# A hybrid diffusion step on one core: query-key norm sums in pool ps2, a weight slot released later, two adaLN slabs moved to the bank change

## The chip, the cores and the metric

The kernel runs on one core of a Trainium2 chip. The metric is the device time of one execution in microseconds (us); the time given for a kernel is the median of its runs. TensorE is called PE here, VectorE DVE, ScalarE ACT, GpSimd POOL and SyncE SP, as in the profile.

## The reference

One inference step of a network of two layers on 640 tokens of width 1024: 512 of a sample and 128 of a prompt. Each layer is FFN1 (SwiGLU, 2816 wide), a mixer, FFN2; each is preceded by a norm that is modulated by `shift`, `scale` and followed by a `gate` (adaLN: nine vectors per layer, from `silu(cond) @ w_ada + b_ada`).

```python
x = x + 0.5 * gate1 * swiglu(mod(rmsnorm(x)))
x = x + gate2 * mixer(mod(rmsnorm(x)))
x = x + 0.5 * gate3 * swiglu(mod(rmsnorm(x)))
# mixer of layer 0
q, k, v, xb, gb = split(h @ w_in)            # 5 x 512 columns
q = rms_norm(q per head of 64, q_g) / 8;  k = rms_norm(k per head of 64, k_g)
y = concat(attention(q, k, v), rglru(xb) * gelu(gb)) @ w_out
# mixer of layer 1: real part of a 2-D DFT, then @ w_out
```

The change lies in layer 0: the norm of `q` and `k`, the opening of the mixer and its out projection.

## The kernel before

**Tiling.** The channels lie on the 128 partitions; the tokens are two halves of 320 (`HT`). Every product of activations and weights is computed from a high and a low part of each operand, as three matmuls (`mm3`, L276 to L284, PE's line L283: high by high, low by high, high by low). A weight unit of 128x1024 arrives by a transfer from SP in a staging buffer `st`, ACT copies its high part (`whi`, L177), DVE subtracts for the low part (`wlo`, L182). Which unit is split when is decided by `prep`, `unit` and `done`: `done` gives a weight slot back, and the split of the next unit is issued there.

**Order.** Nothing reorders the program: each engine runs its instructions in the order in which the Python code issues them, and a wait of one instruction holds all behind it on its engine.

**adaLN.** `w_ada` comes in 144 slabs of 128x1024. `fill` (L312) issues the four matmuls of a slab (L329), which add to an accumulator `ada_ps`, a bank of `ps2`. Eight slabs make one modulation vector; after the eighth, `ada_finish` evacuates the accumulator on ACT (`adaev`, L342), and `ada_end` (L355), called at the next use of any such vector or two slabs later, turns it by two transposes on PE (`adaT`). Slabs are spread over the program by calls of `fill`, as filler for PE. FFN1 of layer 0 ends with 44 used; attention takes up to number 80.

**PSUM.** Of eight banks, pool `ps2` has two, which `bank2` (L105) hands out in turn to the accumulator, norm sums and others; pool `ps` has six, as six single banks or, after `psum(True)` (L92), as three pairs. The mixer of layer 0 runs with pairs.

**The mixer of layer 0** (`mixer0`). FFN1 ends in `down_last`: 16 products `pd` (two halves by eight blocks of 128 channels), each added to `x` on DVE by `x_update` (L383) and followed by the step of the next norm that `after` issues. In the second half every second block hands its weight slot back with `done`. Then the projection: 20 units of `w_in` in the order `IN_ORDER`, each a pair of banks `pj`, one for each half of the tokens. The first three units run together for the first half while the norm of the second half is computed (`norm_a`: sums `nst` on PE, L404, then on DVE from L417 on; `norm_b`). After a unit its evacuation is issued. For `q` and `k` that is `qk_norm` (L1089), a generator: it copies and squares on ACT, and later, in the middle of another unit, issues on PE a sum of squares over each head's 64 channels for either half (`ss`, a product with the block matrix `bones`, L1102), on ACT a table load, Ln and Exp (L1103 to L1107), on POOL a square (L1108), and on DVE (L1110 to L1121) the rest. There are eight such pairs of sums, four of `q` and four of `k`. Between them run the steps of the recurrent unit `lru` (L1037, gates on PE at L1050). After the projection comes `attention` (L1277), with the first blocks of the out projection at its end (`out_ahead` L910, `out_last` L933). Between these two the pool `ps` changes back to single banks: this is the bank change.

Of the kernel before, what the change touches and what calls it, by code (L numbers as in the profile page):

```python
# [11 lines left out]
AF = mybir.ActivationFunctionType  # L12
ALU = mybir.AluOpType
# [9 lines left out]
HT = 320  # L23
SPL = TS - HT
EPS = 1e-6
# [17 lines left out]
class Kern:  # L43
# [687 lines left out]
    def ffn_body(self, l, i, fills, qfills, after, mid, late):  # L731
        nc = self.nc
        gate = self.gate(l, i)
        self.begun = None

        def evac(f, h, pg, pu):
            sg = self.t2.tile([P, HT], F32, tag="y", name="sg", bufs=3)
            nc.scalar.activation(out=sg, in_=pg[:, :HT], func=AF.Silu)
            nc.vector.tensor_tensor(out=sg, in0=sg, in1=pu[:, :HT], op=ALU.mult)
            self.g_split(f, h, sg)  # L740

        def step(n):
            for _ in range(n):
                next(norm, 0)

        if fills:
            us = [self.unit() for _ in range(4)]
            for h in range(2):
                ps = [self.bank("pg") for _ in us]
                for n, j in self.mm_side([p[:, :HT] for p in ps], us, h, 0 if h else LAG):  # L750
                    if j == 3 and h == 0 and n < 4 and (l, i) != (1, 2):
                        self.flush()
                        self.load()
                    elif j == 3:
                        self.prep(self.n_use + 1, 1)
                    if j == 3 and h == 0:
                        if n == 1:
                            if not self.normed:
                                self.norm_a(1)
                            norm = self.norm_steps(1, l, i, True)  # L760
                        elif n == 4:
                            step(3)
                    elif j == 3:
                        step(1)
                        if n < 4:
                            self.fill(fills.pop(0))
                    if (n, j, h) == (EQ, 3, 1):
                        self.quad(2, 0, True)
                    if (n, j, h) == (6, 3, 1):
                        step(9)  # L770
                        self.t_end()
                    if n == 6 and j % 2:
                        evac(j // 2, h, *ps[j - 1:j + 1])
                    if n == 6 and h:
                        self.done(MOST)
                step(2)
            step(9)
            self.t_end()
        else:
            self.ffn_start(evac)  # L780
        f = 2
        for bi, nb in enumerate(BLK):
            end = min(sum(BLK[:bi + 1]) + 1, NF)
            while f < end:
                self.quad(f, qfills.pop(0))
                next(mid, None)
                f += 1
            if bi == 0:
                self.ada_end()
            fs = range(sum(BLK[:bi]), sum(BLK[:bi + 1]))  # L790
            if bi == len(BLK) - 1:
                if late:
                    late()
                self.down_last(fs, gate, after)
            else:
                for c in range(0, KD, 2):
                    w = self.unit()
                    for j in range(2):
                        for h in range(2):
                            p = self.bank("pd")  # L800
                            self.down(p, w, j, h, fs, fs)
                            self.x_update(h, c + j, p, gate)
                    self.done()
# [3 lines left out]
        self.mm3(p[:, 0:HT], w, k, [self.gpart(f, h) for f in now], first=now[0] == fs[0],  # L807
                 last=now[-1] == fs[-1])

    def down_last(self, fs, gate, after):  # L810


        ws = [self.unit() for _ in range(4)]
        self.prep(self.n_use + self.LS)
        order = [(h, c) for h in range(2) for c in range(8)]
        ps = {}
        for n, (h, c) in enumerate(order):
            if n < 4:
                ps[n] = self.bank("pd")
                self.down(ps[n], ws[c // 2], c % 2, h, fs, fs[:-1])  # L820
        for n, (h, c) in enumerate(order):
            p = ps.pop(n, None)
            if p is None:
                p = self.bank("pd")
                self.down(p, ws[c // 2], c % 2, h, fs, fs)
            else:
                self.down(p, ws[c // 2], c % 2, h, fs, fs[-1:])
            self.x_update(h, c, p, gate)
            after(h, c)
            if h and c % 2:  # L830
                self.done()

    def quad(self, f, fills, begin=False):

# [75 lines left out]
    def out_ahead(self, gate, after):  # L910

        (w, p), v = self.ahead, self.unit()
        b = self.pair("w1")

        def end(h):
            self.mm3(p[:, h, 0:HT], w, (3,), [self.h[h][3]], first=False)
            self.x_update(h, 0, p[:, h], gate)
            after(h, 0)

        def whole(h):  # L920
            ks = (7, 6, 5, 4, 0, 1, 2, 3)
            self.mm3(b[:, h, 0:HT], v, ks, [self.h[h][k] for k in ks])
            self.x_update(h, 1, b[:, h], gate)
            after(h, 1)

        end(0)
        whole(0)
        end(1)
        self.done()
        whole(1)  # L930
        self.done()

    def out_last(self, xs, gate, after, c0=0):  # L933
# [155 lines left out]
    def qk_norm(self, which, c, ps):  # L1089

        nc, t2 = self.nc, self.t2
        raw, sq, y = [None] * 2, [None] * 2, [None] * 2
        for h in range(2):
            raw[h] = t2.tile([P, HT], F32, tag=f"acc{h}", name="raw", bufs=1)
            sq[h] = t2.tile([P, HT], F32, tag="sq", name="qsq")
            nc.scalar.activation(out=raw[h], in_=ps[:, h, 0:HT], func=AF.Copy)
            nc.scalar.activation(out=sq[h], in_=raw[h], func=AF.Square)
        yield
        yield
        ss = self.pair("ss")  # L1100
        for h in range(2):
            nc.tensor.matmul(ss[:, h, 0:HT], lhsT=self.bones, rhs=sq[h], start=True, stop=True)  # L1102
        nc.scalar.preload_act_table_set("natural_log_exp_and_others")  # L1103
        for h in range(2):
            y[h] = t2.tile([P, HT], F32, tag="y", name="qy", bufs=3)
            nc.scalar.activation(out=y[h], in_=ss[:, h, 0:HT], func=AF.Ln, scale=1.0 / 64, bias=self.eps)
            nc.scalar.activation(out=y[h], in_=y[h], func=AF.Exp, scale=-0.5)  # L1107
            nc.gpsimd.tensor_tensor(out=sq[h], in0=y[h], in1=y[h], op=ALU.mult)  # L1108
        for h, r0, r1 in ((0, 0, 5), (1, 5, 8)):
            nc.vector.scalar_tensor_tensor(out=sq[h], in0=ss[:, h, 0:HT], scalar=64 * EPS, in1=sq[h], op0=ALU.add, op1=ALU.mult)  # L1110
            nc.vector.tensor_scalar(out=sq[h], in0=sq[h], scalar1=-0.5 / 64, scalar2=1.5, op0=ALU.mult, op1=ALU.add)
            nc.vector.scalar_tensor_tensor(out=y[h], in0=raw[h], scalar=self.qk_g[:, which:which + 1], in1=y[h],
                                           op0=ALU.mult, op1=ALU.mult)
            m = 64 * (r1 - r0)
            if which == 0:
                v = lambda t: t[:, 0:m].rearrange("p (r j c) -> p r j c", j=4, c=16)
                o = self.qs[c][:, 0:TS].rearrange("p (j r c) -> p r j c", j=4, c=16)[:, r0:r1]
            else:
                v = lambda t: t[:, 0:m].rearrange("p (r c) -> p r c", c=64)
                o = self.kt[c][:, r0:r1, 8:72]  # L1120
            nc.vector.tensor_tensor(out=o, in0=v(y[h]), in1=v(sq[h]), op=ALU.mult)  # L1121
        o = self.qs[c][:, TS:] if which == 0 else self.kp[c]
        nc.vector.tensor_tensor(out=o, in0=y[1][:, SPL:], in1=sq[1][:, SPL:], op=ALU.mult)
# [153 lines left out]
    def attention(self, early):  # L1277
        nc, ap, nb, cks, cvs = self.nc, self.ap, self.nb, self.cks, self.cvs
# [89 lines left out]
        for s in range(n + 3):  # L1368
            if 0 <= s - 2 < n:
                B(*tiles[s - 2])  # L1370
            self.fill(min(1, 80 - self.s_use))
            if 0 <= s - 1 < n:
                N(*tiles[s - 1])
            if s < n:
                c, j = tiles[s]
# [8 lines left out]
                    if j == 3:  # L1384
                        self.cache_load(c + 1)
            next(early, None)
            self.fill(min(1, 80 - self.s_use))
            if s >= n and s - n < 2:
                ahead(s - n)
            if 0 <= s - 3 < n:  # L1390
# [477 lines left out]
```

## Time and profile before

| | us |
|---|---|
| median of 3 runs (2276.57 to 2277.95) | 2277.17 |
| the profiled execution | 2276.42 |
| its span in the profile | 2274.6 |
| PE busy | 2219.0 (98%) |
| PE's weight loads | 2106.3 (93%) |
| DVE busy | 1539.6 (68%) |
| ACT busy | 993.2 (44%) |
| POOL busy | 949.1 (42%) |

The mean granted clock of PE is 0.995 of full speed. Of the span, 1.8 us of the profiled execution's time lie outside it. Matmuls overlap in the records, so a row of PE can last longer than the step to the next one. An "x4" behind a row counts the records that it groups; a float32 matmul that is not split leaves two records.

### The profile page before, as it was taken

How to read it: one execution, taken by the hardware profiler on the slowest of the kernel's cores; microseconds unless marked ns; L12 is line 12 of the kernel's file. 1: busy time of each engine (PE TensorE's matmuls, PEld its weight loads, DVE VectorE, ACT ScalarE, POOL GpSimd, SP SyncE). 2: the span in 40 equal slices, each digit the busy share in tenths (PEclk: the TensorE clock that was granted, in tenths of full speed). 3: DMA queues.
4: the chain of work that ended last, by engine and by line, in shares of the span. 5: the costliest groups of instructions: out<-in, count | busy, mean ns of one | idle time of the engine just before them, and what ended most of it. 6: DMA issues, size and time to landing. Idle time of an engine off the chain costs nothing.

```text
span 2274.6 us, 39868 instructions
## 1 busy us (share of the span) xinstructions
PE 2219.0 (98%) x15534; PEld 2106.3 (93%) x15534; DVE 1539.6 (68%) x2871; ACT 993.2 (44%) x1792; POOL 949.1 (42%) x830
## 2 busy tenths in 40 slices
PE   7999999999999999999999999999999999999999
PEld 5899999999995889999999989999999889999999
DVE  6777677666865368666666786666667777666665
ACT  4433333357766444333333453333335453333332
POOL 2544544440023235444444454444443744444441
PEclk9999999999999999999999999999999999999999
DMA  7432333311229333233322243223231422222221
GB/s 291 138 119 88 102 101 107 119 65 57 65 80 320 102 135 107 102 108 107 99 98 82 94 148 130 96 100 112 101 104 54 139 84 84 82 79 84 84 91 56
DMA packets 75508, 245.44 MB, mean 108 GB/s; under 512 B 8884, under 2 KB 13236, under 8 KB 75320
## 3 DMA queue, kind: packets, MB, share of 16 engines
q1 hardware_dynamic: 74168, 241.28, 31.2%
q8 instruction: 123, 2.02, 0.3%
q10 hardware_dynamic: 1152, 1.61, 0.2%
q14 instruction: 65, 0.53, 0.1%
HBM read 239.71 MB, written 3.15 MB: 107 GB/s over the span
## 4 chain that ended last, share of the span: by engine, by line
PE 80%; DVE 11%; ACT 5%; issue 2%; POOL 2%; DMA 0%; ACTq 0%; DVEq 0%; SPq 0%; POOLq 0%
PE q L283 40%; PE pd L283 26%; PE pj L283 5%; PE ada L329 2%; DVE wlo L182 2%; DVE tl L173 1%; PE pg L283 1%; DVE hl L501 1%; ACT hh L487 1%; PE gt L1050 1%; PE pos L1599 1%; DVE x L383 1%; PE w L283 1%; PE S L1303 1%; PE PT L1329 0%
## 5 line engine op out<-in xcount | busy, mean ns | idle before, releaser
L182 DVE TENSOR_TENSOR wlo<-st,whi 128x1024 fp32r<-128x1024 f32 (+2 forms) x401 | 500.3, 1258 | 17.3 <-ACT whi L177 16.7
L177 ACT ACTIVATE whi<-st 128x1024 fp32r<-128x1024 f32 (+2 forms) x405 | 398.5, 991 | 216.2 <-POOL st L233 141.6
L283 PE MATMUL pd<-g,whi 128*128 128x320 f32 x1536 | 347.4, 311 | 2.1 <-DVE x L383 2.0
L383 DVE SCALAR_TENSOR_TENSOR x<-pd,mods,x 128x320 f32<-128x320 f32 (+2 forms) x690 | 260.9, 431 | 96.2 <-PE pd L283 95.9
L283 PE MATMUL q<-hh,whi 128*128 128x320 f32 x960 | 300.9, 313 | 1.0 <-DVE u L838 1.0
L283 PE MATMUL q<-hh,wlo 128*128 128x320 f32 x960 | 296.8, 309 | 2.9 <-DVE wlo L182 2.9
L283 PE MATMUL q<-th,whi 128*128 128x320 f32 x960 | 297.2, 310 | 2.3 <-DVE sg L838 2.3
L283 PE MATMUL q<-th,wlo 128*128 128x320 f32 x960 | 296.5, 309 | 0.0
L283 PE MATMUL q<-hl,whi 128*128 128x320 f32 x960 | 296.3, 309 | 0.0
L283 PE MATMUL q<-tl,whi 128*128 128x320 f32 x960 | 296.1, 308 | 0.0
L838 POOL TENSOR_TENSOR u<-u,u 128x320 f32<-128x320 f32 x80 | 106.0, 1325 | 423.1 <-DVE u L838 369.5
L232 POOL TENSOR_TENSOR st<-sums,st 128x512 f32<-128x512 f32 x80 | 125.0, 1563 | 368.6 <-DVE wlo L182 359.2
L283 PEld LDWEIGHTS pd<-g,whi 128*128 128x128 f32 x1536 | 256.8, 188 | 6.6 <-DVE x L383 3.0
L283 PE MATMUL pd<-g,wlo 128*128 128x320 f32 x768 | 236.9, 308 | 0.0
L283 PE MATMUL pd<-hh,whi 128*128 128x320 f32 x736 | 229.1, 311 | 0.9 <-DVE x L383 0.9
L283 PE MATMUL pd<-hl,whi 128*128 128x320 f32 x736 | 227.8, 310 | 0.0
L283 PE MATMUL pd<-hh,wlo 128*128 128x320 f32 x736 | 227.6, 309 | 0.0
L283 PEld LDWEIGHTS q<-hh,whi 128*128 128x128 f32 x960 | 180.2, 188 | 17.0 <-issue 9.9
L839 ACT ACTIVATE sg<-sg 128x320 f32<-128x320 f32 x160 | 75.4, 471 | 271.7 <-DVE sg L838 271.7
L283 PEld LDWEIGHTS q<-th,whi 128*128 128x128 f32 x960 | 180.2, 188 | 5.6 <-issue 3.2
L283 PEld LDWEIGHTS q<-hh,wlo 128*128 128x128 f32 x960 | 180.2, 188 | 3.7 <-DVE wlo L182 3.7
L283 PEld LDWEIGHTS q<-th,wlo 128*128 128x128 f32 x960 | 180.4, 188 | 0.0
(339 smaller groups left out, 5013.0 us busy)
## 6 DMA issues: line engine op xcount, KB each, us to landing
st<-w_ada SPq DMA_DIRECT2D x144, 512.0 KB, 4.9
st<-ffn_gate SPq DMA_DIRECT2D x88, 512.0 KB, 3.5
st<-ffn_up SPq DMA_DIRECT2D x88, 512.0 KB, 3.6
st<-ffn_down SPq DMA_DIRECT2D x96, 384.0 KB, 3.0
st<-w_in SPq DMA_DIRECT2D x20, 512.0 KB, 3.5
st<-ffn_down SPq DMA_DIRECT2D x16, 512.0 KB, 3.5
st<-w_out_ab SPq DMA_DIRECT2D x8, 512.0 KB, 3.7
st<-w_out_c SPq DMA_DIRECT2D x8, 512.0 KB, 3.5
```

Of the source, the lines that this page charges most:

```text
L173: (eng or self.nc.vector).tensor_tensor(out=lo, in0=src, in1=hi.bitcast(F32), op=ALU.subtract)
L177: self.nc.scalar.activation(out=hi, in_=src, func=AF.Copy)
L182: self.low.tensor_tensor(out=lo, in0=src, in1=hi.bitcast(F32), op=ALU.subtract)
L232: self.nc.gpsimd.tensor_tensor(out=s[:, 0:512], in0=it.s1, in1=s[:, 0:512], op=ALU.subtract)
L283: self.nc.tensor.matmul(out, lhsT=l, rhs=r, start=first and j == 0, stop=last and j == len(ops) - 1)
L329: nc.tensor.matmul(self.ada_ps[32 * j:32 * j + 32, 0:256], lhsT=self.s_sb[:, k, :], rhs=t[:, 256 * j:256 * j + 256], start=k == 0, stop=k ...
L383: self.nc.vector.scalar_tensor_tensor(out=self.x[h][c][:, sl], in0=ps[:, sl], scalar=gate[:, c, r:r + 1], in1=self.x[h][c][:, sl], op0=ALU ...
L487: nc.scalar.activation(out=hi, in_=y, func=AF.Copy)
L501: (self.nc.vector if h or c % 2 else self.nc.gpsimd).tensor_tensor(out=hl, in0=y, in1=hh.bitcast(F32), op=ALU.subtract)
L838: tt = lambda e, o, a, b, op=ALU.add: e.tensor_tensor(out=o, in0=a, in1=b, op=op)
L839: cp = lambda o, p, fn=AF.Copy: nc.scalar.activation(out=o, in_=p, func=fn)
L1050: nc.tensor.matmul(g[:, s, 0:322], lhsT=wt[:, d, j, :], rhs=xc[:, 322 * s:322 * s + 322], start=True, stop=True)
```

## The change

Three edits.

1. In `qk_norm` the two sums of squares, one for each half of the tokens, are no longer the two banks of a pair of pool `ps`, but two tiles of one bank each from `ps2`, by `bank2`.
2. In `down_last`, only in FFN1 of layer 0, the third hand-back of a weight slot in the second half (block 5) is left out and made up for at the end.
3. In attention the slabs go up to number 78 in place of 80; slabs 78 and 79 are issued in `out_ahead`, behind its last product.

```diff
-                self.down_last(fs, gate, after)
+                self.down_last(fs, gate, after, l == i == 0)
...
-    def down_last(self, fs, gate, after):
+    def down_last(self, fs, gate, after, hold=False):
...
-            if h and c % 2:
+            if h and c % 2 and (c != 5 or not hold):
                 self.done()
+        if hold:
+            self.done()
...
         whole(1)
+        self.fill(2)
         self.done()
...
-        ss = self.pair("ss")
+        ss = [self.bank2("ss") for _ in range(2)]
         for h in range(2):
-            nc.tensor.matmul(ss[:, h, 0:HT], lhsT=self.bones, rhs=sq[h], start=True, stop=True)
+            nc.tensor.matmul(ss[h][:, 0:HT], lhsT=self.bones, rhs=sq[h], start=True, stop=True)
...
-            nc.scalar.activation(out=y[h], in_=ss[:, h, 0:HT], func=AF.Ln, scale=1.0 / 64, bias=self.eps)
+            nc.scalar.activation(out=y[h], in_=ss[h][:, 0:HT], func=AF.Ln, scale=1.0 / 64, bias=self.eps)
...
-            nc.vector.scalar_tensor_tensor(out=sq[h], in0=ss[:, h, 0:HT], scalar=64 * EPS, in1=sq[h], op0=ALU.add, op1=ALU.mult)
+            nc.vector.scalar_tensor_tensor(out=sq[h], in0=ss[h][:, 0:HT], scalar=64 * EPS, in1=sq[h], op0=ALU.add, op1=ALU.mult)
...
-            self.fill(min(1, 80 - self.s_use))
+            self.fill(min(1, 78 - self.s_use))
```

The last pair of lines stands twice in `attention`. The line numbers of the changed kernel are those of before, plus 1 from L811 on, plus 3 from L832 and plus 4 from L931: the sums at L1102 are now at L1106, DVE's first read of them moves from L1110 to L1114.

**The sums, on PE.** The first of the eight pairs, in the middle of the fourth unit of the projection; `ss` are the sums, `pj` the projection. Each row names in brackets the engines and transfer queues that its instruction waits for. Before:

```order
L283 MATMUL pj_5288<-hh7_101,wlo1_70 128x320
L1102 MATMUL ss_5540<-qsq_5465,bones_5228 128x320 [waits DMAHW4_49,DMAHW2_49,DMAHW5_49,DMAHW1_49,DMAHW7_49,DMAHW0_49,Activation_49]
L1102 MATMUL ss_5540<-qsq_5469,bones_5228 128x320 [waits Activation_49]
L283 MATMUL pj_5561<-hh0_87,whi0_67 128x320 [waits PE_49,Activation_49]
L283 MATMUL pj_5561<-hl0_88,whi0_67 128x320
```

Now:

```order
L283 MATMUL pj_5288<-hh7_101,wlo1_70 128x320
L1106 MATMUL ss_5540<-qsq_5465,bones_5228 128x320 [waits DMAHW2_49,DMAHW4_49,DMAHW1_49,DMAHW5_49,DMAHW0_49,DMAHW7_49,PE_49,Activation_49]
L1106 MATMUL ss_5541<-qsq_5469,bones_5228 128x320 [waits DVE_49]
L283 MATMUL pj_5562<-hh0_87,whi0_67 128x320
L283 MATMUL pj_5562<-hl0_88,whi0_67 128x320
```

The second sum waits for DVE in place of ACT, and the second half of the unit follows behind it. The accumulator `ada_4264` is the tile of `ps2` that is open meanwhile: its last slab before the projection, and its first one after, which is in attention, stand in PE's order now as they did before:

```order
L329 MATMUL ada_4264<-st0_157,s_sb_112 32x256 [waits Pool_49]
L329 MATMUL ada_4264<-st0_157,s_sb_112 32x256
```

```order
L329 MATMUL ada_4264<-st2_66,s_sb_112 32x256 [waits DMAHW4_49]
L329 MATMUL ada_4264<-st2_66,s_sb_112 32x256 x3
```

**The opening, on DVE.** The last norm steps of FFN1's end and the low half of two weight units; `hl` is the low part of the normed input, `x` the residual. Before:

```order
L498 SCALAR_TENSOR_TENSOR hl_94<-y,mods,hh_93 128x320
L182 TENSOR_TENSOR wlo_70<-st_64,whi_69 128x1024
L383 SCALAR_TENSOR_TENSOR x_86<-pd,mods,x_86 128x192
L383 SCALAR_TENSOR_TENSOR x_86<-pd,mods,x_86 128x128
L475 SCALAR_TENSOR_TENSOR y<-x_85,sc,nbc 128x320
L383 SCALAR_TENSOR_TENSOR x_86<-pd,mods,x_86 128x192
L383 SCALAR_TENSOR_TENSOR x_86<-pd,mods,x_86 128x128
L479 TENSOR_TENSOR y<-x_85,nbc 128x320
L498 SCALAR_TENSOR_TENSOR hl_98<-y,mods,hh_97 128x320
L475 SCALAR_TENSOR_TENSOR y<-x_85,sc,nbc 128x320
L498 SCALAR_TENSOR_TENSOR hl_102<-y,mods,hh_101 128x320
L182 TENSOR_TENSOR wlo_68<-st_66,whi_67 128x1024
```

Now:

```order
L498 SCALAR_TENSOR_TENSOR hl_94<-y,mods,hh_93 128x320
L383 SCALAR_TENSOR_TENSOR x_86<-pd,mods,x_86 128x192
L383 SCALAR_TENSOR_TENSOR x_86<-pd,mods,x_86 128x128
L475 SCALAR_TENSOR_TENSOR y<-x_85,sc,nbc 128x320
L383 SCALAR_TENSOR_TENSOR x_86<-pd,mods,x_86 128x192
L383 SCALAR_TENSOR_TENSOR x_86<-pd,mods,x_86 128x128
L479 TENSOR_TENSOR y<-x_85,nbc 128x320
L498 SCALAR_TENSOR_TENSOR hl_98<-y,mods,hh_97 128x320
L475 SCALAR_TENSOR_TENSOR y<-x_85,sc,nbc 128x320
L498 SCALAR_TENSOR_TENSOR hl_102<-y,mods,hh_101 128x320
L182 TENSOR_TENSOR wlo_70<-st_64,whi_69 128x1024
L182 TENSOR_TENSOR wlo_68<-st_66,whi_67 128x1024
```

`wlo_70` has moved from between the norm steps to behind the last of them, next to `wlo_68`. On ACT one split (`whi_67`) moves in the same way behind its last norm step for that half. On PE the projection opens with three units in turn, and `wlo_70` is read by its ninth matmul, here the third row:

```order
L283 MATMUL pj_5288<-hh0_87,whi1_69 128x320 [waits Activation_49]
L283 MATMUL pj_5288<-hl0_88,whi1_69 128x320
L283 MATMUL pj_5288<-hh0_87,wlo1_70 128x320 [waits DVE_49]
L283 MATMUL pj_5286<-hh1_89,whi2_71 128x320
L283 MATMUL pj_5286<-hl1_90,whi2_71 128x320
```

**The bank change, on PE.** The end of attention and of `out_ahead`; `w` is the product of `out_ahead`, `pd` the first of `out_last`. Before, the transposes of the last vector stand in front of the end of `out_ahead`:

```order
L1342 MATMUL o<-pt,cv 64x128 x2
L1342 MATMUL op<-pt,vts 64x128 x2
L355 MATMUL adaT<-ident,adaev 128x128 x2
L283 MATMUL w_7807<-hh_93,whi_71 128x320
L283 MATMUL w_7807<-hl_94,whi_71 128x320
```

and `out_ahead` is followed by `pd` directly:

```order
L283 MATMUL w_7889<-hl_94,whi_75 128x320
L283 MATMUL w_7889<-hh_93,wlo_76 128x320
L283 MATMUL pd<-hh_101,whi_69 128x320
L283 MATMUL pd<-hl_102,whi_69 128x320
L283 MATMUL pd<-hh_101,wlo_70 128x320
```

Now the two slabs and the transposes stand between them:

```order
L283 MATMUL w_7883<-hl_94,whi_75 128x320
L283 MATMUL w_7883<-hh_93,wlo_76 128x320
L329 MATMUL ada<-st_6789,s_sb 32x256 x4
L329 MATMUL ada<-st_6790,s_sb 32x256 x4
L355 MATMUL adaT<-ident,adaev 128x128 x2
L283 MATMUL pd<-hh_101,whi_69 128x320
```

The transposes (`adaT`) wait for the evacuation of the vector on ACT, which in turn waits for the second slab.

## Rows read from the trace of the kernel before

**Rows 1.** Page, part 4: chain that ended last, share of the span by engine.
```profile
PE 80%; DVE 11%; ACT 5%; issue 2%; POOL 2%; DMA 0%; ACTq 0%; DVEq 0%; SPq 0%; POOLq 0%
```

**Rows 2.** Windows, 528:684: length, then PE, PEld, DVE, ACT, POOL busy, clock, DMA.
```profile
528.00:684.00 156.00, 154.30 (x973) 145.44 (x973) 113.19 (x201) 111.81 (x185) 20.32 (x23) 1.00 0.22 72
```

**Rows 3.** Waits of PE, 490:760: total us, times, longest us.
```profile
PE gt L1050 <- DVE qsq L1110: 1.6, 1, 1.6
```

**Rows 4.** Timeline of PE, L1102: start us, us, engine, line, operation.
```profile
535.65 1.24 PE L1102 MATMUL ss<-qsq,bones 128*128 128x320 f32 x4
...
607.14 1.24 PE L1102 MATMUL ss<-qsq,bones 128*128 128x320 f32 x4
...
623.38 1.24 PE L1102 MATMUL ss<-qsq,bones 128*128 128x320 f32 x4
...
651.77 1.24 PE L1102 MATMUL ss<-qsq,bones 128*128 128x320 f32 x4
...
666.92 1.24 PE L1102 MATMUL ss<-qsq,bones 128*128 128x320 f32 x4
...
675.04 1.24 PE L1102 MATMUL ss<-qsq,bones 128*128 128x320 f32 x4
```

**Rows 5.** Timeline of DVE, L1110, the first read of each pair.
```profile
539.92 0.49 DVE L1110 SCALAR_TENSOR_TENSOR qsq<-ss,qsq 128x320 f32<-128x320 f32 x1 [1.40 <-POOL qsq L1108]
...
612.23 0.48 DVE L1110 SCALAR_TENSOR_TENSOR qsq<-ss,qsq 128x320 f32<-128x320 f32 x1
...
633.14 0.48 DVE L1110 SCALAR_TENSOR_TENSOR qsq<-ss,qsq 128x320 f32<-128x320 f32 x1
...
662.24 0.48 DVE L1110 SCALAR_TENSOR_TENSOR qsq<-ss,qsq 128x320 f32<-128x320 f32 x1
...
670.38 0.49 DVE L1110 SCALAR_TENSOR_TENSOR qsq<-ss,qsq 128x320 f32<-128x320 f32 x1 [0.61 <-POOL qsq L1108]
...
680.76 0.49 DVE L1110 SCALAR_TENSOR_TENSOR qsq<-ss,qsq 128x320 f32<-128x320 f32 x1 [6.07 <-POOL qsq L1108]
```

**Rows 6.** Timelines of DVE and ACT, with the idle time ahead.
```profile
619.18 0.83 DVE L1071 SCALAR_TENSOR_TENSOR tz<-tz,lt 128x644 f32<-128x644 f32 x1 [2.57 <-ACT lt L1068]
...
668.20 0.53 ACT L1106 ACTIVATE qy<-ss,eps 128x320 f32<-128x320 f32 x1 [0.44 <-PE ss L1102]
```

**Rows 7.** Timelines of DVE (three) and PE (three), the opening of the projection.
```profile
505.97 1.90 DVE L182 TENSOR_TENSOR wlo<-st,whi 128x1024 fp32r<-128x1024 f32 x1
...
512.81 1.22 DVE L182 TENSOR_TENSOR wlo<-st,whi 128x1024 fp32r<-128x1024 f32 x1
...
514.44 0.14 DVE L417 TENSOR_SCALAR nst<-nst 128x3 f32<-128x3 f32 x1
...
509.65 0.39 PE L283 MATMUL pj<-hh,whi 128*128 128x320 f32 x1 [1.64 <-ACT hh L477]
...
510.90 0.31 PE L283 MATMUL pj<-hh,wlo 128*128 128x320 f32 x1
...
513.40 0.36 PE L404 MATMUL nst<-ones,sq 128*128 128x1 f32 x2
```

**Rows 8.** Timelines of PE (two) and ACT, attention and bank change.
```profile
773.71 0.39 PE L283 MATMUL pd<-hh,whi 128*128 128x320 f32 x1 [0.86 <-DVE x L383]
...
744.55 0.64 PE L329 MATMUL ada<-st,s_sb 128*32 128x256 f32 x8
...
773.60 0.47 ACT L393 ACTIVATE sq<-x 128x320 f32<-128x320 f32 x1 [2.56 <-DVE x L383]
```

**Rows 9.** Windows 70.10:73.30 and 510:513.2, columns as in rows 2; timeline of PE ahead.
```profile
70.10:73.30 3.20, 3.20 (x16) 2.83 (x18) 2.63 (x4) 0.47 (x1) 3.12 (x4) 0.50 0.02 9
510.00:513.20 3.20, 3.20 (x27) 3.20 (x25) 1.79 (x4) 1.65 (x4) 3.13 (x20) 1.00 0.17 67
...
68.90 0.42 PE L283 MATMUL pg<-hh,whi 128*128 128x320 f32 x1 [1.58 <-ACT hh L487]
```

More of the change, by code (lines that the diff above doesn't have):

```diff
@@ L1386, in attention @@
             next(early, None)
-            self.fill(min(1, 80 - self.s_use))
+            self.fill(min(1, 78 - self.s_use))
             if s >= n and s - n < 2:
```

## The prediction

> **What bounds the kernel now.** I read the chain of waits of the page first. 80% of it lies on PE, 11% on DVE and 5% on ACT [rows 1]: TensorE sets the time, and whatever makes PE stand still is paid in full unless PE waits there already. Then the window over layer 0's projection, from the first sums of squares to the last, where most of the change lies: PE is busy 154.30 of 156.00 us at granted clock 1.00, while DVE and ACT are at 113 and 112 [rows 2]. So PE has no slack, the others a quarter. PE's waits from the end of FFN1 to the out projection come third: a single one belongs to the sums, 1.6 us at a gate matmul that needed the pair of banks which DVE still read (`qsq`) [rows 3]. Last, the timelines: where PE does the eight pairs of sums [rows 4], and when DVE does its first read of each pair [rows 5]. DVE's read comes 3.5 to 10.5 us after the sums began; today that lateness costs nearly nothing, as PE goes on with the next projection.
>
> **Edit 1, the sums.** A pair of sums is four records in 1.24 us of 0.43 each, so they start (1.24 − 0.43)/3 = 0.27 apart and the second half's sum starts 0.54 after the first [rows 4]. The change takes each half's sum from pool `ps2`, which has two banks. One of them isn't free: the accumulator `ada` of modulation vector 5 is opened at the end of FFN1 and gets its last slabs in attention (the order rows), since 16 + 4 + 24 = 44 slabs are used when the mixer starts and 44 = 5·8 + 4. So both sums of a pair use the one bank that is left, and the second waits until DVE has read the first; the order shows that wait on DVE where there was one on ACT. PE is in order: behind the second sum stand the next half unit of the projection and the gates. Ahead of DVE's read stand, in turn, ACT's table load, Ln and Exp, POOL's square, and whatever ACT and DVE have queued ahead of them.
>
> A wait is worth: end of DVE's first read, less start of the sums, less 0.54, plus 0.06 for the signal (my estimate, of the order of the 0.02 to 0.1 us between rows that release each other). From the rows [rows 4, 5]: 539.92 + 0.49 + 0.06 − 535.65 − 0.54 = 4.28 for the first pair, and likewise 5.09, 9.76, 10.47, 3.47 and 5.73 for the fourth to the eighth; the second and third, whose rows repeat the pattern and don't stand there, give 6.43 and 4.78. Sum 50.0.
>
> Do ACT and DVE catch up while PE stands? Mostly not, for their lateness is a chain that PE's own gates start, a fixed time after PE issued them. For the fifth wait it is partly otherwise: DVE's run up to that read begins at 619.18, released by ACT's root [rows 6], and ACT's work for it came from gates just behind the fourth sums. These come 5.1 us later, but ACT then has only the second half's norm ahead of them: the run starts some 3.0 later, so −2.1 (bounds 0 and −5.1). At the seventh ACT stood idle for 0.44 and waited for both sums [rows 6]; with one sum to wait for, −0.8. Together **+47.1**. If every wait shrank to the bare chain as the seventh shows it (Ln at 668.20 to the read's end at 670.87, with the sum and signal 2.7), it would be 8 × 2.7 = 22: the lower bound; 50.0 is the upper. I take 47.1, as six of the eight are work that PE starts.
>
> The gates' wait on the pair of banks goes: **−1.6** [rows 3]. ACT's second Ln now waits for the second sum; what is queued behind it on ACT and DVE waits too, up to the same 2.7 us per pair, but PE is then already on its way and a quarter of their time is free. POOL's and SP's rows keep their order.
>
> **Edit 2, the slot handed back later.** On DVE the low half of the opening's third weight unit, `wlo_70`, moves from 505.97 to behind the last norm step, and ACT's split of a later unit moves behind its own, as the order shows [rows 7]. The 1.90 us it took leave the way of the last two x updates, so PE's first projection matmul starts about 0.8 earlier than 509.65. But PE's ninth matmul there reads `wlo_70`. The last norm step ended at 512.81; 0.8 to 1.9 earlier and a split of 1.22 give 512.1 to 513.2, I take 512.6. Before, that ninth stood at 510.90: 1.7 later. DVE's norm of the other half started at 514.44, when PE's sums for it had been done (513.40 + 0.36) for 0.7 us [rows 7]; so it starts 1.0 later, and PE waits for its results further on: **+1.0** (bounds −0.8, if the norm isn't late, and +2.3, if the split runs to 513.2 and the slack is used up otherwise). The transfer that refills the staging buffer goes out about 4 us later; PE waits for no transfer in the whole stretch of that view, and the unit is needed only after the three opening ones. Without that cover those 4 us would be the price.
>
> **Edit 3, two slabs at the bank change.** A slab takes PE 0.64 [rows 8]. Two leave attention: PE waits there on ACT and DVE between its pieces, so little of their 1.3 comes back; I take −0.3. They go into the wait of 0.86 that ends at 773.71. By themselves they would overrun it by 0.4, but modulation vector 9 (slabs 72 to 79) is then complete only there: its evacuation stands on ACT behind the square that runs at 773.60 for 0.47 [rows 8], takes about as long itself (an estimate from that square), and two transposes (0.27, the spacing of two records of the sums) must follow before `pd`. So 773.60 + 0.47 + 0.47 + 0.27 = 774.81 instead of 773.71: +1.1. Net **+0.8** (bounds −0.2, if attention gives back all of the 1.3, and +1.4).
>
> **The clock.** After an idle time of 1.58 us at 68.90 the granted clock stood at 0.50 from 70.10 to 73.30 [rows 9]. After 1.59 us at the gates it stayed at 1.00 [rows 2, 3], and after 1.64 at 509.65 it did too [rows 7, 9]. So 1.6 us is a border case, and waits of 2.7 to 10 us lie beyond it. A stretch of 3.4 us at 0.50 loses 1.7. I take six falls of eight: **+10.2** (bounds 0, and two such stretches after each wait, 8 × 3.4 = 27).
>
> The Trainium skill, page "TensorE: Matmul & The Clock Gate", section "HAM oscillation — how this bites in real kernels", tells of this: an engine that waits between its bursts of matmuls falls to half rate in each wait and starts every burst there. By that rule all eight waits are followed by a fall, 8 × 1.7 = 13.6 in place of 10.2, and the time would be 2337; it speaks against the change. The row at 68.90 agrees, the other two don't reach it.
>
> **Sum:** 47.1 − 1.6 + 1.0 + 0.8 + 10.2 = +57.5 on the profiled execution's 2276.42, so **2334**. That execution lies 0.75 below the median of the runs shown; the range takes this in.
>
> **The rivals.**
> (a) *The second bank is free.* If vector 5's accumulator were done before 535, the sums would take one bank each and PE would only lose the 1.6 at the gates: 2276.4 − 1.6 + 1.8 from edits 2 and 3 = 2276.6, not slower. What decides is whether the bank is free from the first sums on. For it: the two sums are separate tiles. Against: the accumulator's rows in the order and the wait on DVE. Chance 0.03.
> (b) *ACT and DVE catch up.* The waits shrink towards the bare chain: 22 − 1.6 + 1.8 = +22, and from no fall to a fall after each (13.6) that is 2298 to 2312. For it: a quarter of DVE and ACT is free [rows 2], and DVE idles 2.57 ahead of 619.18 [rows 6]. Against: the runs ahead of the fifth and sixth reads hang on gates that PE issues. Chance 0.17.
> (c) *The whole price, and long falls.* 50.0 − 1.6 + 1.8 + 27 = +77: 2353. For it: long waits, eight times, and the row at 68.90. Against: a stretch of full projection follows each wait. Chance 0.18.
> (d) *No falls:* 2276.4 + 47.3 = 2324, inside the forecast's own range.
>
> **How the numbers follow.** Forecast 0.62 (2318 to 2345). The range from 2303 to 2352 takes in most of (b) and reaches to (c), leaving about 0.1 on each side. A measurement of this kernel tells about 0.2% (4.6 us) from no change. Faster than that needs a gain that no edit has: 0.02. Within it is (a) alone: 0.02. Slower has the rest, 0.96.
>
> **What would show it.** Right: eight waits of PE on DVE's first read at the second sum, 45 us or so together, the longest at the fifth and sixth; DVE's and ACT's first halves unchanged in length; the wait at the gates gone; PE waiting on `wlo_70` after eight matmuls of the projection; the granted clock at 0.5 behind most of the waits; the stretch from the end of attention to the first `pd` a microsecond longer. Wrong: no DVE wait at the sums (a); waits that are all near 3 us (b); a clock of 1.00 through the projection, which gives (d).

## The result and the profile after

The changed kernel takes 2338.95 us (median of 4 runs, 2337.63 to 2339.31), the one before 2277.44 beside it: a ratio of 1.0269 (95% interval 1.0256 to 1.0281). The profiled execution took 2337.63 us with a span of 2335.8, that is 61.2 more than the one before in both. The forecast was +57.5.

Of the page, the chain of waits by engine, which answers to [rows 1]:

```profile
PE 79%; DVE 11%; ACT 6%; issue 2%; POOL 1%; DMA 0%; ACTq 0%; DVEq 0%; SPq 0%; POOLq 0%
```

It hardly differs, and that is worth seeing: shares of the whole span don't show 61 us that lie in a tenth of it. The window over the projection does. It runs from as far ahead of the first sums to as far behind attention's first transposes (those of `vt`) as the one of [rows 2], with the same columns:

```profile
531.25:744.05 212.80, 171.29 (x973) 158.12 (x973) 114.84 (x202) 112.53 (x185) 17.90 (x23) 0.89 0.17 57
```

212.80 us in place of 156.00, with the same 973 records of matmuls. PE is busy for 171.29 of them, so it stands idle for 41.5 where it stood for 1.7; and it is busy 17.0 longer than before for the same work, at a mean granted clock of 0.89. So the loss has two parts, waits and a lower clock, and DVE and ACT (115 and 113 us, where they had 113 and 112) have hardly more to do than they had. PE's waits from the opening to the out projection (total us, times, longest) name the first part:

```profile
PE ss L1106 <- DVE qsq L1114: 41.4, 8, 9.8
...
PE pj L283 <- DVE wlo L182: 2.5, 1, 2.5
...
PE pj L283 <- DVE x L383: 0.9, 1, 0.9
```

The wait at the gates of [rows 3] is gone, and eight waits at the second sum have come. The last row is the wait ahead of the projection's first matmul, which before was 1.64 us for ACT [rows 7]. The timeline of PE at the sums: each pair is now two rows of two records; all eight second sums stand here, and three of the first ones:

```profile
538.90 0.70 PE L1106 MATMUL ss<-qsq,bones 128*128 128x320 f32 x2
...
543.70 1.43 PE L1106 MATMUL ss<-qsq,bones 128*128 128x320 f32 x2 [4.10 <-DVE qsq L1114]
...
571.26 1.44 PE L1106 MATMUL ss<-qsq,bones 128*128 128x320 f32 x2 [6.25 <-DVE qsq L1114]
...
604.11 1.43 PE L1106 MATMUL ss<-qsq,bones 128*128 128x320 f32 x2 [4.60 <-DVE qsq L1114]
...
636.44 1.43 PE L1106 MATMUL ss<-qsq,bones 128*128 128x320 f32 x2 [4.60 <-DVE qsq L1114]
...
655.16 0.70 PE L1106 MATMUL ss<-qsq,bones 128*128 128x320 f32 x2
...
661.34 1.43 PE L1106 MATMUL ss<-qsq,bones 128*128 128x320 f32 x2 [5.48 <-DVE qsq L1114]
...
700.28 1.44 PE L1106 MATMUL ss<-qsq,bones 128*128 128x320 f32 x2 [9.76 <-DVE qsq L1114]
...
719.88 0.81 PE L1106 MATMUL ss<-qsq,bones 128*128 128x320 f32 x2 [2.44 <-DVE qsq L1114]
...
729.11 0.70 PE L1106 MATMUL ss<-qsq,bones 128*128 128x320 f32 x2
...
733.98 0.81 PE L1106 MATMUL ss<-qsq,bones 128*128 128x320 f32 x2 [4.17 <-DVE qsq L1114]
```

What a wait costs is the second sum's start less the first's less 0.54: 543.70 − 538.90 − 0.54 = 4.26, then 6.41, 4.77, 4.76, 5.64, 9.92, 2.59 and 4.33, together 42.7. The lengths of the rows tell of the second part: a pair of records that took 0.70 before the wait takes 1.43 behind six of the waits, at half clock. Behind the last two it takes 0.81, and the clock falls a little later. Windows right behind four of PE's waits, with the granted clock in the third column from the right:

```profile
513.30:516.10 2.80, 2.78 (x10) 2.78 (x11) 1.47 (x4) 0.00 (x0) 0.00 (x0) 0.50 0.59 184
543.70:547.10 3.40, 3.40 (x11) 3.01 (x12) 1.33 (x4) 1.89 (x3) 0.72 (x1) 0.51 0.21 84
636.40:642.60 6.20, 6.16 (x17) 4.97 (x18) 3.85 (x9) 4.59 (x6) 0.72 (x1) 0.50 0.15 45
721.10:724.50 3.40, 3.40 (x15) 3.40 (x14) 1.92 (x5) 1.52 (x5) 2.67 (x4) 0.50 0.02 5
```

The first is behind a wait in the opening, the others behind the first, fourth and seventh sums. All eight waits at the sums are followed by such a stretch at 0.50, the shortest some 3.1 us long and the longest 6.2. What they cost can be read without the clock: from a second sum to the next first sum it is 564.31 − 543.70 = 20.61 us, where it was 555.15 − 535.65 − 0.54 = 18.96, so 1.65; the other seven give 1.54, 2.12, 3.02, 0.63 (with the 1.6 of the gates gone, so 2.2), 1.86, 1.65 and 1.65. Together +14.1, or 15.7 for the clock and −1.6 for the gates.

So the 61.2 us lie here:

| stretch | us |
|---|---|
| ahead of the edits: the norm's sums for the first half, in FFN1's end (492.60 against 492.10) | +0.5 |
| opening, from there to the first sum (538.90 against 535.65) | +2.75 |
| eight waits at the second sums | +42.7 |
| between the sums: half clock +15.7, gates −1.6 | +14.1 |
| attention and bank change, up to `pd` | +0.4 |
| the rest of the program | +0.8 |

In the first row nothing is edited up to there; executions differ by that much and more in such places, as the next section shows. The two rows that it is read from, the one of before first:

```profile
492.10 0.28 PE L404 MATMUL nst<-ones,acc 128*128 128x1 f32 x2
...
492.60 0.28 PE L404 MATMUL nst<-ones,acc 128*128 128x1 f32 x2
```

### The profile page after: what moved, and what is told of

It is laid out like the page before. It is cut to its first block, busy times and chain, and to the rows that moved or that the text cites. A ratio compares the mean times of both kernels' runs of the same rounds, so it can differ in the third digit from the quotient of the medians.

```text
span 2335.8 us, 39857 instructions
## 1 busy us (share of the span) xinstructions
PE 2237.5 (96%) x15534; PEld 2121.5 (91%) x15534; DVE 1539.8 (66%) x2871; ACT 994.0 (43%) x1792; POOL 945.5 (40%) x830
## 4 chain that ended last, share of the span: by engine, by line
PE 79%; DVE 11%; ACT 6%; issue 2%; POOL 1%; DMA 0%; ACTq 0%; DVEq 0%; SPq 0%; POOLq 0%
PE q L283 40%; PE pd L283 25%; PE pj L283 5%; PE ada L329 2%; DVE wlo L182 2%; DVE tl L173 1%; PE pg L283 1%; ACT hh L487 1%; DVE hl L501 1%; PE gt L1054 1%; PE pos L1603 1%; PE w L283 1%; DVE x L383 1%; PE ss L1106 0%; DVE y L479 0%
```

## The experiments

For the runs below a short stretch says more than the whole time: from the first sum to attention's first transposes of `sx` (`PT`, the row that waits 0.33 us for `hh` of L172). Before it is 688.29 − 535.65 = 152.64 us, in the changed kernel 748.34 − 538.90 = 209.44. The start of the projection itself differs by up to 2.0 us (509.12 to 511.12) even among runs whose program is the same up to there, which has no part in this stretch.

| run | first sum to `PT`, us | ratio to before (95%) |
|---|---|---|
| change | 209.4 | 1.0269 (1.0256 to 1.0281) |
| edit1_alone | 210.1 | 1.0249 (1.0235 to 1.0263) |
| edit2_alone | 152.7 | 1.0014 (1.0005 to 1.0022) |
| edit3_alone | 152.7 | 0.9998 (0.9989 to 1.0007) |
| filled_waits | 196.4 | 1.0208 (1.0194 to 1.0222) |
| second_sum_later | 180.7 | 1.0145 (1.0131 to 1.0159) |
| before_free_bank | 152.7 | 1.0008 (0.9999 to 1.0017) |
| edit1_free_bank | 150.8 | 1.0003 (0.9995 to 1.0012) |
| change_free_bank | 150.8 | 1.0017 (1.0008 to 1.0026) |

**Each edit alone.** Three kernels with one edit of the diff each.

> Edit 1 alone: only the two sums of squares go to two tiles of pool ps2; edits 2 and 3 are left out. Theory A (both sums use one bank of ps2, since the accumulator holds the other, so PE stands eight times and its clock falls after each wait): the eight waits of the changed kernel, 42.7 us together by their starts, the lost time at half clock behind them, 15.7, and the wait at the gates that is gone, -1.6: +56.8, so about 2334 against a before of 2277.4. Theory B (the opening's late weight half and the moved slabs push the projection's engines out of step, and the waits are long because of that): well under half of it, under 2305.

> Edit 2 alone: only the hand-back of the slot is later. Theory A: PE waits 2.5 us for the low half of the third unit, the clock falls behind that wait, and the sums for the other half's norm come 3.8 us later, of which 0.6 were slack: +3.2, about 2280.6 (2279.5 to 2281.5). If the fall is not from this wait: +1.8, 2279.2. Theory B: more than 10, since the projection runs late from here on.

> Edit 3 alone: only the two slabs are moved. Theory A: the stretch from the last piece of out_ahead to pd is 0.9 us longer and attention 0.5 shorter, with up to 0.8 further on: +0.4 to +1.2, 2277.8 to 2278.6. Theory B of an effect on the order of slabs further on: 2 us or more.

Edit 1 alone took 2336.14 us (2334.04 to 2336.88) beside a before of 2278.37, so 57.8 more where 56.8 were expected. Its waits:

```profile
PE ss L1102 <- DVE qsq L1110: 42.6, 8, 9.8
```

42.6 us, with no other edit in the program: theory B, that edits 2 and 3 make them long, is out. Edit 2 alone gave +0.14%, which is 3.2 us, as expected, though the interval (1.1 to 5.0 us) would also take in the +1.8 without a fall. Its trace decides: it has the wait of 2.53 us on `wlo`, the clock at 0.50 from 512.2 to 515.5 behind it, and its first sum 29.5 us after the projection's start, in place of 26.0; counted from the norm's sums in FFN1's end, as in the table above, that is 2.7 us later. Edit 3 alone can't be told from nothing by the ratio. In its trace the transposes wait 0.54 us for the evacuation, as in the change, but a wait of PE on ACT in attention is 1.98 us long where before it is 0.8, and the clock falls behind it:

```profile
748.05 0.99 PE L1330 MATMUL PT<-ident,sx 128*128 128x128 f32 x6 [1.98 <-ACT pt L1333]
...
748.70:752.00 3.30, 3.30 (x23) 2.33 (x20) 2.13 (x8) 3.13 (x9) 2.46 (x2) 0.50 0.37 97
```

From `PT` to `pd` it is 1.2 us longer than before (774.41 − 687.75 = 86.66 against 85.42), the upper end of what was expected; in the change the same wait is 1.63, no fall follows, and the same stretch is only 0.4 longer.

**The clock apart from the waits.** To keep PE busy in the waits without taking a wait away, matmuls are put ahead of each second sum whose result isn't read:

```diff
         ss = [self.bank2("ss") for _ in range(2)]
+        d, x = self.pair("dm"), self.h[0][0][0]
         for h in range(2):
+            if h:
+                for _ in range(self.DM.pop(0)):
+                    nc.tensor.matmul(d[:, 0, 0:HT], lhsT=x[:, 0:P], rhs=x, start=True, stop=True)
             nc.tensor.matmul(ss[h][:, 0:HT], lhsT=self.bones, rhs=sq[h], start=True, stop=True)
```

> The whole change, and ahead of each second sum PE is given 26, 39, 29, 29, 46, 60, 15 and 26 extra matmuls at 0.147 us whose result nobody reads, to fill most of the wait. Theory A (a fall of the clock follows each wait and costs 14 to 16 us in all): the clock stays at 1.00 through most of the projection and the time falls by 10 to 15, to 2324 to 2329, although PE does 40 us more work; the fifth wait grows from 5.6 to some 7.7, as the slow stretch ahead of it, in which DVE caught up, is gone. Rival C (the half clock in the records costs nothing, the waits are all of the price): no change, or longer by what the extra matmuls overrun, 2339 to 2343.

It took 2326.72 us: 12.2 less than the change, for 270 matmuls more. PE's waits at the second sum, a window over the third and fourth of them, and the fifth pair on PE:

```profile
PE ss L1110 <- DVE qsq L1118: 3.9, 8, 1.0
...
600.00:650.00 50.00, 49.30 (x316) 46.98 (x315) 36.59 (x64) 36.32 (x51) 2.88 (x4) 1.00 0.12 38
...
649.97 0.70 PE L1110 MATMUL ss<-qsq,bones 128*128 128x320 f32 x2
...
658.20 0.81 PE L1110 MATMUL ss<-qsq,bones 128*128 128x320 f32 x2 [0.78 <-DVE qsq L1118]
```

What PE stands idle ahead of the second sums is down to 3.9 us, the window has a clock of 1.00, as has all of the stretch up to `PT`, and the second records take the 0.81 that go with it. Yet the second sum comes no sooner: the waits by their starts are 4.26, 6.42, 4.77, 4.77, 7.69, 9.93, 2.61 and 4.33, 44.8 in all. Less the gates' 1.6 that is 43.2 of the 43.8 us that the stretch is longer than before, so next to nothing is left for the clock. The stretch is 13.0 us shorter than in the change (196.44 against 209.44) although its waits are 2.1 longer: 15.1 us for the clock, beside the 15.7 read above. So the half clock costs what its stretches show, and rival C is out. The fifth wait is 658.20 − 649.97 − 0.54 = 7.69 in place of 5.64: in the changed kernel PE's slow stretch of 6.2 us behind the fourth sums had given DVE and ACT time to catch up. Edit1_alone lies between: 1.6 us were lost at half clock behind its fourth sums (3.0 in the change), and its fifth wait is 6.84.

**The bank.** What if no accumulator is open through the projection? FFN1 of layer 0 does four slabs less, so that vector 5 isn't begun; attention does them.

```diff
-    FILLS = {"0ffn1": ((), (4, 0) + (2,) * 2 + (1,) * 16),
+    FILLS = {"0ffn1": ((), (4, 0) + (2,) * 2 + (1,) * 12 + (0,) * 4),
```

It was put on the kernel before (a control), on that with edit 1, and on the whole change.

> Control: the kernel before, but FFN1 of layer 0 does 20 slabs in place of 24 (none with its last four pairs), so 40 are used when the mixer starts and no accumulator is open through the projection; attention does the four more. All theories: within 2 us of before, 2275.5 to 2279.5; PE is saved 4 x 0.6 = 2.4 us in FFN1 and gets them back in attention, where a part lies in waits.

> Edit 1 on that control: two tiles of ps2 for the sums, with both banks free. Theory A (the price is the shared bank): no wait of PE on DVE's first read, and the 1.6 us at the gates are gone: control -1.6 (-2.5 to 0). Rival D (the price lies in splitting the pair itself: ACT and DVE wait for two tiles apart): control +20 or more.

> The whole change with both banks free, by the same 20 slabs in FFN1. Theory A: the run before this one plus edits 2 and 3, some +3.6, so control +2 (0 to +4). Rival D: control +25 or more, up to the +61 of the change.

The control took 2278.03 us, edit 1 on it 2279.32 (2275.19 to 2280.90), the whole change on it 2281.06, each beside a before of 2277.77. The 57 us are gone: the same two tiles of `ps2`, the same instructions behind them, and the stretch is 1.85 us shorter than before. All of that lies between the fifth and the sixth sums, where the wait at the gates was; it was worth a little more than its 1.6, so that the clock's part in the change is rather 16.0 than 15.7. Rival D, that splitting the pair is what costs, is out; what costs is that both tiles share a bank. On edit1_free_bank's timeline of PE the pair is again one row of four records without a wait, and the gates' wait has gone; but then comes a row of attention, and two windows around it:

```profile
532.89 1.24 PE L1102 MATMUL ss<-qsq,bones 128*128 128x320 f32 x4
...
694.02 0.64 PE L329 MATMUL ada<-st,s_sb 128*32 128x256 f32 x8 [2.31 <-ACT adaev L342]
...
693.00:697.00 4.00, 2.98 (x30) 1.64 (x32) 1.43 (x7) 2.54 (x8) 3.24 (x4) 0.76 0.66 231
...
697.00:700.00 3.00, 3.00 (x26) 2.09 (x23) 0.73 (x4) 0.81 (x1) 0.00 (x0) 0.75 0.66 229
```

The same place in the control, with a window:

```profile
694.33 0.64 PE L329 MATMUL ada<-st,s_sb 128*32 128x256 f32 x8 [1.57 <-ACT adaev L342]
...
694.00:698.00 4.00, 3.67 (x48) 2.26 (x48) 2.45 (x8) 2.19 (x8) 3.49 (x5) 1.00 0.76 274
```

This is where most of the 1.85 us went. Counted from the first sum, PE came to a new accumulator 1.5 us earlier than in the control, and ACT's evacuation of the last one only 0.7 earlier. So the wait for it grew from 1.57 to 2.31 us, and behind the longer one the clock fell (0.76 and 0.75), where it had stayed at 1.00. From the first sum to `pd` 0.7 us are left (774.30 − 532.89 = 241.41 against 242.12 in the control). The expected −1.6 against the control is in the stretch, but not in the time: the medians are 2279.32 and 2278.03. The whole change with the free bank, 3.0 above the control, lies within its forecast.

**The queue.** The wait costs because the projection stands behind it. In the next kernel the second half's sum and norm are issued one step later, behind half a unit of the projection (for all pairs but one, the seventh, whose buffers the next pair needs). ACT's table load is then issued once for each half.

```diff
-        ss = [self.bank2("ss") for _ in range(2)]
-        for h in range(2):
-            nc.tensor.matmul(ss[h][:, 0:HT], lhsT=self.bones, rhs=sq[h], start=True, stop=True)
...
+        for h, r0, r1 in ((0, 0, 5), (1, 5, 8)):
+            if h and (which or c):
+                yield
+            ss[h] = self.bank2("ss")
+            nc.tensor.matmul(ss[h][:, 0:HT], lhsT=self.bones, rhs=sq[h], start=True, stop=True)
```

> The whole change, one bank as in it, but for seven of the eight pairs the second half's sum and norm are issued one step later, behind the next half unit of the projection (24 matmuls, 3.5 us) and what stands there. Theory A (a wait costs because the projection stands behind it in PE's queue): each of the seven waits loses 3.5 us or vanishes: 42.7 becomes about 18, and some four falls are saved: 2338.9 - 25 - 7 = 2307 (2298 to 2318). Rival E (ACT's extra table loads and the second norm make DVE's reads later, and the waits move along): 2325 or more.

2311.07 us (2308.36 to 2312.18), and 28.0 us instead of 56.8 more than before in the stretch; 19.9 us of waits are left of 41.4. Two of its waits on PE's timeline, and the window behind each:

```profile
595.36 0.81 PE L1109 MATMUL ss<-qsq,bones 128*128 128x320 f32 x2 [1.09 <-DVE qsq L1115]
...
624.20 0.81 PE L1109 MATMUL ss<-qsq,bones 128*128 128x320 f32 x2 [2.04 <-DVE qsq L1115]
...
595.36:598.76 3.40, 3.40 (x21) 3.24 (x22) 1.99 (x4) 3.33 (x5) 0.00 (x0) 1.00 0.02 5
...
624.20:627.60 3.40, 3.40 (x14) 3.24 (x15) 1.99 (x4) 3.34 (x4) 0.00 (x0) 0.66 0.02 9
```

A wait of 1.09 us leaves the clock at 1.00, one of 2.04 doesn't. Of the eight, those of 0.58, 0.67 and 1.09 us had no fall behind them, those of 2.04 to 6.25 had one. Theory A holds within its range, if at its upper half: the fourth and fifth waits lost 2.6 and 1.4 us in place of 3.5.

**A version that beats both?** edit1_free_bank gains in the projection and loses in attention. So in attention one call of `fill` is left out each time a vector is complete, on that kernel, on the kernel before, and on that kernel with edit 3 as well (there with 78 in place of 80).

```diff
+        seen = [self.s_use]
+
+        def fill1():
+            if self.s_use % 8 == 0 and self.s_use not in seen:
+                seen.append(self.s_use)
+            else:
+                self.fill(min(1, 80 - self.s_use))
...
-            self.fill(min(1, 80 - self.s_use))
+            fill1()
```

> Edit 1 with both banks free, as edit1_free_bank, and in attention one call of fill is left out each time a modulation vector is complete (the slabs come later, none is lost), so that the next accumulator isn't asked for while ACT still evacuates the last. Theory F (edit1_free_bank gained 1.9 us in the projection and lost it in attention, where PE waited 2.3 us for that evacuation and its clock fell behind the wait): that wait and the fall go, -3 to -5 against edit1_free_bank, so 2273 to 2275 beside a before of 2277.5. Rival G (attention has no slack: what isn't filled is waited for at another place): no change against edit1_free_bank, within 1.

> The kernel before with the same calls left out in attention, its 24 slabs in FFN1 and its sums as they were. Theory F: the waits of 0.7 and 1.04 us for the evacuation go, and no fall stood behind them: -1 to -2, 2275.5 to 2276.5. Rival G: no change.

> edit1_free_skip with edit 3, the two slabs at the bank change. Theory A: edit 3 costs nothing to 1 us: 0 to +1 against edit1_free_skip. If the two slabs are covered by the wait of 0.9 there: -1.

Beside a before of 2277.52 they took 2275.86 (ratio 0.9996, 0.9987 to 1.0005), 2277.18 (0.9998, 0.9990 to 1.0007) and 2278.67 (1.0007, 0.9998 to 1.0016). None can be told from before, so no version here is known to beat it. Theory F doesn't hold in before_skip: the waits of 0.7 and 1.04 for the evacuation are gone, but PE now waits 1.03 us at transposes for DVE's `mods`, and from the first sum to `pd` only 0.4 are gained; there it is as rival G has it. In edit1_free_skip it does: the wait in attention is 1.15 us with no fall behind it, and `pd` begins at 770.28, 4.0 us ahead of edit1_free_bank and 3.4 ahead of before [rows 8]. This kernel is still 3.4 ahead of before at the norm sums of layer 1's mixer (1280.04 against 1283.42). Then the windows of edit1_free_skip from there on read

```profile
1280.00:1285.00 5.00, 4.43 (x25) 3.94 (x26) 3.62 (x8) 3.47 (x7) 1.70 (x2) 0.76 0.12 48
1285.00:1290.00 5.00, 5.00 (x22) 5.00 (x21) 2.00 (x11) 0.00 (x0) 0.00 (x0) 0.55 0.91 318
```

and those of before, likewise from its norm sums on,

```profile
1283.40:1288.40 5.00, 4.97 (x25) 4.75 (x26) 3.64 (x8) 3.44 (x6) 1.67 (x2) 0.67 0.11 44
1288.40:1293.40 5.00, 5.00 (x35) 4.81 (x34) 2.46 (x12) 0.00 (x0) 0.00 (x0) 0.99 0.89 318
```

Both have waits of about half a microsecond there, and both fall to half clock; but in the first PE waits again inside the slow stretch, 0.53 us at 1284.47, and the stretch lasts some 7 us, in the other some 3.4. Two of the 3.4 us gained go there, and 0.8 more further on. The last forecast, on edit 3, failed: +2.8 by the medians, with intervals that overlap, and the trace shows where. In edit13_free_skip `pd` comes at 773.18, 2.9 us later than in edit1_free_skip:

```profile
772.84 0.69 PE L355 MATMUL adaT<-ident,adaev 128*128 128x128 f32 x2 [4.89 <-ACT adaev L342]
...
771.10 1.06 ACT L177 ACTIVATE whi<-st 128x1024 fp32r<-128x1024 f32 x1 [3.96 <-DMA st<-w_out_ab]
```

The transposes wait 4.89 us for the evacuation, which stands on ACT behind the split of a weight unit that waited 3.96 us for its transfer, and the clock is at 0.50 from 770.1 to 776.9. So the two slabs are cheap at the bank change only while nothing holds ACT there; why the transfer comes late in that kernel was not tried.

## Why the prediction was right

**What held.** The mechanism did, in each link: both sums on one bank, since the accumulator has the other (edit1_free_bank); PE standing in its queue until DVE's first read (second_sum_later); ACT's and DVE's lateness as a chain that PE's own work starts, so that most waits come out as the queues stood. The first three were forecast to 0.02 us (4.28, 6.43, 4.78 against 4.26, 6.41, 4.77). Rival (a) was a matter of the bank and got its answer in the runs that free it (with the free bank the whole change is 3.3 us slower by the medians, more than (a)'s +0.2, as the opening costs more than forecast); rival (b) stays out, as the waits are 42.7 and not 22, and (c), as the stretches at half clock cost 15.7 and not 27.

**What was off**, term by term, against +57.5:

- *The waits, 47.1 forecast, 42.7 measured.* Two terms make up 3.4 of the 4.4. The fifth was 5.64 for a forecast of 7.66. The correction for ACT's work was right, 7.69 in filled_waits where the clock doesn't fall; what was left out is that a slow PE also gives the others time. The eighth was 4.33 for 5.73, and 4.33 in filled_waits too. There POOL had its own queue, on the timeline of before

```profile
675.83 4.21 POOL L1274 TENSOR_TENSOR nb<-mk,u 128x256 f32<-128x256 f32 x6 [4.13 <-DMA u<-rpb]
...
680.00 1.40 POOL L1108 TENSOR_TENSOR qsq<-qy 128x320 f32<-128x320 f32 x2
```

and of after, where POOL's work for attention's bias was done by then:

```profile
732.68 0.72 POOL L1112 TENSOR_TENSOR qsq<-qy 128x320 f32<-128x320 f32 x1 [4.78 <-ACT qy L1111]
```

The square (L1108, now L1112) had stood behind `nb`. The forecast counted "whatever ACT and DVE have queued ahead of them", and no queue of POOL's. Most of the rest is the sixth (9.92 for 10.47) and the fourth (4.76 for 5.09), for which the runs show no reason.

- *The clock, 10.2 forecast, 15.7 measured.* Six falls of eight were taken, at 1.7. It was eight of eight, and three of them, behind the third, fourth and fifth sums, cost 2.1, 3.0 and 2.2, as PE worked 4.4, 6.2 and 5.2 us at 0.50 behind them. The Trainium skill, page "TensorE: Matmul & The Clock Gate", section "HAM oscillation — how this bites in real kernels", tells of a kernel in which each wait for a transfer, of some 3 to 5 us, is followed by a fall. The traces agree, eight times of eight, and do so for waits of PE down to 2.44 us; the 13.6 that this gave was nearer than my 10.2.

- *The opening, +1.0 forecast, +2.75 measured (+3.25 with the 0.5 ahead of it).* The mechanism was as told. PE at the ninth matmul and at the norm's sums, and DVE at the two low halves:

```profile
513.32 0.64 PE L283 MATMUL pj<-hh,wlo 128*128 128x320 f32 x1 [2.53 <-DVE wlo L182]
...
516.15 0.36 PE L404 MATMUL nst<-ones,acc 128*128 128x1 f32 x2
...
512.05 2.35 DVE L182 TENSOR_TENSOR wlo<-st,whi 128x1024 fp32r<-128x1024 f32 x2
```

and the first of the norm's sums before:

```profile
512.37 0.28 PE L404 MATMUL nst<-ones,acc 128*128 128x1 f32 x2
```

From the norm's sums for the first half to PE's start it is 16.78 us (492.60 to 509.38), where it was 17.55 (492.10 to 509.65): 0.77 sooner, as the 0.8 forecast. DVE began the two splits (one row here) at 512.05, `wlo_70` first, and PE went on at 513.32. Less the 0.5, the ninth matmul came 1.9 later, for 1.7 forecast. The slack of DVE's norm, 0.7, was right too. What the forecast left out is that a fall followed this wait of 2.53 us as well, which I had charged to the sums alone: PE worked 2.8 us at half clock, and lost 1.4. So the norm's sums came 516.15 − 512.37 = 3.8 later, and DVE's norm 3.2 (517.67 against 514.44), all with the 0.5.

- *The bank change, +0.8 forecast, +0.4 measured.* The order of events is the one described:

```profile
832.31 1.07 PE L329 MATMUL ada<-st,s_sb 128*32 128x256 f32 x16
...
833.92 0.44 PE L355 MATMUL adaT<-ident,adaev 128*128 128x128 f32 x2 [0.54 <-ACT adaev L342]
...
834.12 0.40 PE L283 MATMUL pd<-hh,whi 128*128 128x320 f32 x1
...
833.50 0.37 ACT L342 ACTIVATE adaev<-ada 128x256 f32<-128x256 f32 x1
```

The evacuation ran at 833.50 for 0.37, the transposes 0.20 ahead of `pd`, and from the last product of `out_ahead` to `pd` it is 0.9 us longer. But attention gave back 0.5 and not 0.3. That is in part luck: in edit3_alone, where the clock fell once more in attention, it gave back nothing and the term was +1.2.

The sum came out near the mark partly because the misses have both signs: −4.4, +5.5, +1.75, −0.4 and +1.3 outside the stretches that the edits touch (0.5 ahead of them and 0.8 further on) make the +3.7 by which it was short.

## What to carry to other kernels

Before a tile is given a bank of its own, count what else in that pool is open at the time: two tiles in a ring of two banks are one bank when an accumulator holds the other, and then the second write waits for the first one's last read. The price is read ahead of time from the trace, as the distance between the write and that read, taken as the queues stand; add what a stretch at half clock costs in rows of the same trace, for each such wait. And if the tile must wait, what matters is what stands behind it in its engine's queue.

## What the runs showed that I had not expected

- A fall of the clock can come in the middle of a wait and outlast it by 3 to 6 us of work: at the second sums the clock was at 0.50 from about 567.5 on, PE went on at 571.26, and the clock rose at 574.4. In these runs it followed every wait of PE that is named here and lasted 1.98 us or more, and none at the sums of 1.09 or less. In between both occur: the one of 1.57 us in the control and the one of 1.63 in the change had none behind them, while 1.58 us at 68.90 [rows 9] and 1.76 in attention of filled_waits did. And at layer 1's norm sums in before, two waits of 0.48 and 0.42 us (1281.25 and 1283.42) were followed by one.
- A few microseconds gained upstream don't always reach the end: 1.1 of 1.85 us were lost to one longer wait and its fall in attention, and 2 of 3.4 to a slow stretch of 7 us in place of 3.4 behind like waits in layer 1. Whether the earlier arrival decides on the length of such a stretch was not tried. Another execution can change it where neither program nor wait differs: behind the opening's wait of 2.53 us the clock was at 0.50 from 512.9 to 516.3 in the change, and from 515.6 to 522.4 in filled_waits, whose program is the same up to there.
